# When a group's inputs are split, and which engine makes the low parts, in the second feed-forward of a fused diffusion step

## The chip, the cores and the metric

The kernel runs on one core of a Trainium2 chip. A core has a matrix engine (TensorE, PE in the profile; its weight loads are listed as PEld), VectorE (DVE), ScalarE (ACT), GpSimd (POOL), and SyncE (SP), whose queue issues the DMAs. The metric is the device time of one whole execution in microseconds (us); lower is better.

## The reference

One step of a backbone with a single layer (width 1024, hidden width 2816) for 1024 latent and 128 context tokens. All of it is float32. Of the layer, only the last part matters here:

```
x = x + 0.5 * m[2] * swiglu(modulate(x, norm_g[0], m[0], m[1]), *ffn1)
x = x + m[5] * token_mixer(modulate(x, norm_g[1], m[3], m[4]), ...)
x = x + 0.5 * m[8] * swiglu(modulate(x, norm_g[2], m[6], m[7]), *ffn2)
y = rmsnorm(x, final_g)

modulate(x, g, shift, scale) = rmsnorm(x, g) * (1.0 + scale) + shift
swiglu(h, w1, w3, w2)        = (silu(h @ w1) * (h @ w3)) @ w2
```

## The kernel before, in words

**Layout and precision.** Activations are held transposed: 128 features on the partitions, 1152 tokens along the free axis, so x is eight tiles x0 to x7. The tokens are cut into four quarters of 288 (`QUARTERS`), worked through in the order 3, 0, 1, 2 (`QORDER`), so the last one is tokens 576 to 863. A float32 product is made of three passes: each operand is split into a high part (a rounded copy, on ScalarE) and a low part (value minus high part, one subtraction on VectorE or GpSimd), and TensorE adds high x high, high x low and low x high (`mm3`, lines 518 to 520). So for every operand there is a copy and a subtraction before TensorE can use it.

**Second feed-forward, up.** The third residual's norm is applied quarter by quarter by `norm` (a generator; the one for the last quarter is `self.tail`). For each of eight feature tiles k it multiplies x by the reciprocal root (L476, DVE), applies gain and shift (L480, ACT), writes the vector to DRAM (L483), copies the high part (L487, ACT) and subtracts for the low part (L488, POOL). The result, an entry vector, lands in the tiles B. The scratch tile `xn` comes from a ring of four tiles of 128x288 with the tag "sl"; the SiLU results of the blocks below come from the same ring. A second ring, `half`, holds six tiles of 128x576 with the tag "xp".

Three plain blocks come first (`plain_block`, f = 0, 1, 2; 128 hidden units each). A block is two weight tiles (j = 0 for w1, j = 1 for w3) times four quarters, 24 matmuls each, in one of three PSUM banks with the tag "up". For j = 0 ScalarE takes the SiLU (L1723), for j = 1 DVE multiplies the two (L1734) and the result is written to DRAM. The weights come through `load_w` and `hl`: DMA, copy on ACT (L350), subtraction on POOL (L351, 128x1024). `hl` has another branch, home="low", in which the subtraction is made on DVE in two halves of 128x512. While the plain blocks run, a generator `sums` builds sums and differences of the entry vectors from DRAM, in tiles of the ring `half` (L1678 to L1681, then L1684 and L1688 on ACT and DVE), which the fast blocks (from f = 3) need: these use a scheme with seven products in place of eight (`PRODUCTS` is their order). In the first block the last quarter is taken last, since its norm is ready last.

**Second feed-forward, down.** The hidden vectors from f = 3 on are taken in pairs and in three groups (`GROUPS`: 2, 3 and 3 pairs). For each group `down_fast` makes four sweeps (m = 0 to 3), each of seven products (`down_sweep`; matmuls in L2004). A product takes, for both pairs of quarters, n = 2 or 3 pairs of hidden vectors and three passes, so 12 or 18 matmuls. Its result is emptied from the bank on ACT (L1987, L2007) or DVE (L1989, L1991, L2009); some products start on a bank that an earlier one has filled, after that bank was read. Between products `after()` is called. It brings in, among other work, the splits of the inputs: the generator `down_xs` yields one split at a time (load of 128x576 into a tile of `half`, five ahead; copy on ACT, L1968; subtraction on POOL, L1969, or on DVE for every k = 1). A group with three pairs has 21 splits, three for each product. In the first group's first sweep one split is drawn per product; those of the next group are begun at m = 2 (their first five loads) and all drawn in the last sweep, m = 3:

```
if m == KT // 2 - 1 and not last:
    for _ in range(GROUPS[g + 1][1]):
        next(xg, None)
```

The weights of the sweeps are split by `down_ops` (L1942 on ACT, L1943 on DVE; in the last group also sums on POOL, L1937).

**What sets the order.** The program is written as a sequence of instructions, and a planner at build time puts those of each engine in one queue: among the instructions whose inputs and tiles are free by its own estimate of time, the one written first goes first, unless an instruction is pinned. The queue then runs strictly in that order on the chip. So a place in the program is a priority, not a time.

Of the kernel before, what the change touches and what calls it, by code (L numbers as in the profile page):

```python
# [9 lines left out]
F32 = mybir.dt.float32  # L10
# [9 lines left out]
P = 128  # L20
D = 1024
KT = D // P
# [19 lines left out]
QORDER = [QUARTERS[q] for q in QS]  # L42
# [3 lines left out]
GROUPS = (3, 2), (7, 3), (13, 3)  # L46
# [3 lines left out]
def span(c):  # L50

    return c if isinstance(c, tuple) else (c * CW, (c + 1) * CW)


def segs(c):

    lo, hi = span(c)
    r = []
    if lo < TL:
        r.append((lo, min(hi, TL), 0))  # L60
    if hi > TL:
        r.append((max(lo, TL), hi, 1))
    return r
# [30 lines left out]
class Trunk:  # L94
# [354 lines left out]
    def norm(self, c, i):  # L449

        nc = self.nc
        lo, hi = span(c)
        cs = slice(lo, hi)
        rs = self.rs[:, cs]
        if self.mode != "mix":
            rs = self.bank("ps1", "rsp", hi - lo)
        last = self.mode == "mix"
        if last:
            with self.tc.high_priority(offset=600):
                self.stat_end(c, rs)  # L460
        else:
            self.stat_end(c, rs)
        yield
        for k in range(KT):
            t = self.fp.tile([P, hi - lo], F32, tag=self.nt[0], bufs=self.nt[1], name="xn")
            if last:
                for a, b, s in segs(c):
                    v, th, tl = t[:, a - lo : b - lo], self.xh[k][:, a:b], self.xl[k][:, a:b]
                    g, sh = self.gs[:, i, k, s : s + 1], self.modt[:, 3 * i, k, s : s + 1]
                    rv = rs[:, a - lo : b - lo]  # L470
                    nc.vector.scalar_tensor_tensor(v, self.x[k][:, a:b], g, rv, ALU.mult, ALU.mult)
                    nc.scalar.activation(th, v, AF.Identity, bias=sh)
                    nc.vector.scalar_tensor_tensor(tl, v, sh, th, ALU.add, ALU.subtract)
                yield
                continue
            nc.vector.tensor_mul(t, self.x[k][:, cs], rs)  # L476
            for a, b, s in segs(c):
                v = t[:, a - lo : b - lo]
                g, sh = self.gs[:, i, k, s : s + 1], self.modt[:, 3 * i, k, s : s + 1]
                nc.scalar.activation(v, v, AF.Identity, scale=g, bias=sh)  # L480
            if i == 2:
                q, r, j = self.place(c)
                nc.sync.dma_start(self.hd[r, k % 4][:, 2 * (k // 4) + j], t)  # L483
                th, tl = [v[:, k % 4] for v in self.B[q][k // 4]]
            else:
                th, tl = self.xh[k][:, cs], self.xl[k][:, cs]
            nc.scalar.copy(th, t)  # L487
            nc.gpsimd.tensor_sub(tl, t, th)  # L488
            yield

    def place(self, c):
# [278 lines left out]
    def proj_gate(self, i, p, pair):  # L770
# [16 lines left out]
        def put(cs, s):  # L787
            nc.gpsimd.tensor_mul(s, oT[:, cs], s)
            nc.sync.dma_start(self.orec[p][:, cs], s)

        self.later.append(norm)
        for c in ORDER:
            ps = yield from self.proj_g(w, c)
# [1231 lines left out]
    def down_fast(self, w2, X, xg, ops, made, load_x, load_h, split_h, gm, nxt):  # L2025

        S = [self.tt(F32, "su")[:, :T].rearrange("p (m n) -> p m n", m=4) for _ in range(2)]
        rest = [2, *range(PLAIN[1] + 16, NF)]
        pend, ws = [], []
        self.folds = []  # L2030
        for g, (f, n) in enumerate(GROUPS):
            new = {} if g else X
            last = g == len(GROUPS) - 1
            for m in range(KT // 2):
                if m == 2 and not last:
                    new = {}
                    xg = self.down_xs(g + 1, new)
                    next(xg)
                k, raws, xa = 0, [], []
                if g and m in (1, 2):  # L2040
                    xa += [(i, load_x(i)) for i in range(4 * g + 2 * m - 6, 4 * g + 2 * m - 4)]

                def after():
                    nonlocal k
                    if xa and k in (2, 5):
                        i, t = xa.pop(0)
                        for v in range(2):
                            c = ts(v, 2 * QW)
                            self.nc.vector.tensor_add(self.x[i][:, c], t[:, c], self.x[i][:, c])
                    if m == KT // 2 - 1 and not last:  # L2050
                        for _ in range(GROUPS[g + 1][1]):
                            next(xg, None)
                    elif last:
                        for _ in range((0, 0, 1, 2, 1, 1, 1)[k]):
                            self.folds.pop(0)()
                        if m == KT // 2 - 1:
                            if k in (0, 2):
                                raws.append(load_h(k // 2))
                            if k in (1, 3):
                                pend.append(split_h(*raws.pop(0)))  # L2060
                            if k in (0, 2):
                                ws.append(self.load_w(w2[k // 2], 1, D, home=partial(self.tt, F32R)))
                    elif not g and not m:
                        next(xg, None)
                    k += 1

                self.down_sweep(g, m, X, ops, made, gm, S, after)
            X = new
        assert not made
        for f in rest[:2]:  # L2070
            pend.append(split_h(*load_h(f)))
        fs, hs = zip(*pend[:2])
        assert not self.folds
        self.down_group(w2, fs, hs, gm, ws)
        for f in rest[2:]:
            pend.append(split_h(*load_h(f)))
        fs, hs = zip(*pend[2:])
        self.down_last(w2, fs, hs, gm, nxt)

    def ffn_fast(self, l, gm, nxt):  # L2080

        nc = self.nc
# [7 lines left out]
        sums, ops, made = iter(()), iter(()), []  # L2090
        steps = iter(()) if l else self.whole()
        for f in range(plain):
            ws = self.pre[f] if l == 0 and f < 2 else [self.load_w(self.a["w13"][l, f, j], KT, P) for j in range(2)]
            if f == 2 - l:
                for _ in steps if l == 0 else self.tail:
                    pass
                sums = self.sums()
            if f == plain - 1:
                ops = self.fast_ops(l, range(plain, NF))
            n = 0  # L2100

            def after():
                nonlocal n
                if l and f == 0:
                    next(self.tail, None)
                elif f == 1 - l:
                    if n % 2 == 0:
                        next(steps, None)
                elif f:
                    next(sums, None)  # L2110
                if f == plain - 1 and n > 7 and n % 2:
                    made.append(next(ops))
                n += 1

            self.plain_block(l, f, ws, after)
# [4 lines left out]
        pend, ws, raws = [], [], []  # L2120
# [38 lines left out]
        xg = self.down_xs(0, X) if l else None  # L2159
# [52 lines left out]
        for f in range(2, NF):  # L2212
            pend.append(split_h(*load_h(f)))
            if f % 2 and f < NF - 1:
                fs, hs = zip(*pend[:2])
                self.down_group(w2, fs, hs, gm, ws or [load_w2(v) for v in fs])
                pend, ws = pend[2:], None
# [127 lines left out]
```

## Time and profile before

| | us |
|---|---|
| median of three runs | 2864.26 |
| lowest and highest | 2857.67, 2866.94 |
| the profiled execution | 2864.89 |
| its span in the profile | 2862.8 |
| idle of TensorE in front of the matmuls of the plain blocks (L518, L519) | 5.3 |
| idle of TensorE in front of the matmuls of the sweeps (L2004) | 8.2 |

The profile lists for each engine its instructions with the line of the kernel, the tiles written and read ("out<-in"), and the shape. A row of waits names the instruction that waited, the one that released it, the sum in us, the number of waits and the longest. A row of a window gives for a stretch of time the busy time of each engine and the number of its instructions, then the clock granted to TensorE as a share of full speed, the share of the DMA engines that was busy, and GB/s. Matmuls are pipelined: each is listed with about 0.29 us, but one starts every 0.13 us.

### The profile page before, as it was taken

The numbers are of one execution on the slowest core, as the hardware profiler recorded it, in microseconds if no ns is written. First come the engines' busy times: TensorE is split into PE (matmuls) and PEld (weight loads), VectorE is DVE, ScalarE is ACT, GpSimd is POOL, SyncE is SP. The second block draws the span as 40 slices with busy tenths as digits, with TensorE's granted clock in tenths as the row PEclk, the third lists the DMA queues.
The fourth block names the chain that finished last, engine by engine and source line by source line (L and its number), as shares of the span: only waits on it lengthen the run. The fifth ranks groups of instructions, "written<-read, shape, count | busy, mean of one in ns | idle before, by whom it ended". The sixth has DMA issues, their size and how long they took to land. (4 is left out here: it accounts for less than half of the span.)

```text
span 2862.8 us, 55873 instructions
## 1 busy us (share of the span) xinstructions
PE 2776.7 (97%) x21222; PEld 2644.7 (92%) x21222; DVE 2027.9 (71%) x4439; ACT 1333.4 (47%) x2740; POOL 961.3 (34%) x1003
## 2 busy tenths in 40 slices
PE   8999999999999999999999999989999999999998
PEld 7999999999989999889998777689989999999997
DVE  7867777677678787876356677855765676568885
ACT  6523332321176677666545777721642322235332
POOL 0133322544222222222144444532442443423450
PEclk9999999999999999999999999999999999999999
DMA  6743433743112111112512001263543443446631
GB/s 258 225 129 118 132 122 123 261 165 118 62 65 69 49 57 35 54 46 74 174 45 75 16 16 30 82 215 97 181 153 116 147 152 122 126 146 209 204 100 67
DMA packets 218940, 331.76 MB, mean 116 GB/s; under 512 B 24048, under 2 KB 142768, under 8 KB 218672
## 3 DMA queue, kind: packets, MB, share of 16 engines
q1 hardware_dynamic: 218672, 328.20, 35.3%
q8 instruction: 167, 2.74, 0.4%
q14 instruction: 101, 0.83, 0.1%
HBM read 244.93 MB, written 83.18 MB: 115 GB/s over the span
## 5 line engine op out<-in xcount | busy, mean ns | idle before, releaser
L1804 PE MATMUL b<-xo,wo 128*128 128x288 f32 x3552 | 483.6, 295 | 1.1 <-DVE wo L1779 1.1
L1804 PEld LDWEIGHTS b<-xo,wo 128*128 128x128 f32 x3552 | 475.5, 188 | 1.3 <-DVE wo L1779 1.3
L1804 PE MATMUL b<-bh,wo 128*128 128x288 f32 x1776 | 366.4, 295 | 0.0
L518 PE MATMUL mm<-xh,wh 128*128 128x384 f32 x984 | 345.6, 351 | 14.1 <-DVE sg L795 5.2
L520 PE MATMUL mm<-xh,wl 128*128 128x384 f32 x984 | 335.1, 341 | 0.0
L519 PE MATMUL mm<-xl,wh 128*128 128x384 f32 x984 | 334.5, 340 | 0.0
L1804 PEld LDWEIGHTS b<-bh,wo 128*128 128x128 f32 x1776 | 289.2, 188 | 0.1
L547 DVE SCALAR_TENSOR_TENSOR x<-dn,modt,x 128x256 f32<-128x256 f32 (+4 forms) x472 | 225.5, 498 | 88.3 <-PE dn L520 87.0
L1804 PE MATMUL b<-bl,wo 128*128 128x288 f32 x888 | 262.2, 295 | 0.0
L1778 ACT CAST wo<-raw 128x512 fp32r<-128x512 f32 x185 | 114.8, 621 | 204.7 <-issue 85.6
L518 PEld LDWEIGHTS mm<-xh,wh 128*128 128x128 f32 x984 | 187.1, 190 | 22.9 <-DVE sg L795 6.8
L519 PEld LDWEIGHTS mm<-xl,wh 128*128 128x128 f32 x984 | 187.1, 190 | 1.1 <-issue 0.3
L2004 PE MATMUL d<-xd,wd 128*128 128x288 f32 x1344 | 179.7, 295 | 8.2 <-DVE x L1991 4.0
L520 PEld LDWEIGHTS mm<-xh,wl 128*128 128x128 f32 x984 | 187.3, 190 | 0.0
L2004 PEld LDWEIGHTS d<-xd,wd 128*128 128x128 f32 x1344 | 178.5, 188 | 9.3 <-ACT wd L1942 3.6
L1779 DVE TENSOR_TENSOR wo<-raw,wo 128x512 fp32r<-128x512 f32 x185 | 127.4, 689 | 70.9 <-ACT wo L1778 68.0
L390 DVE SCALAR_TENSOR_TENSOR junk<-wada,cb 128x512 bf16<-128x512 f32 x224 | 163.9, 732 | 8.6 <-DMA wada<-in_w_aT 7.8
L1516 POOL TENSOR_TENSOR ehl<-e,ehl 128x512 fp32r<-128x512 f32 x93 | 122.0, 1317 | 141.4 <-ACT ehl L1514 75.9
L1804 PEld LDWEIGHTS b<-bl,wo 128*128 128x128 f32 x888 | 167.3, 188 | 0.0
L351 POOL TENSOR_TENSOR wl<-raw,wh 128x1024 fp32r<-128x1024 f32 (+2 forms) x48 | 95.3, 1986 | 161.6 <-ACT wh L350 142.7
L518 PE MATMUL ps<-bh,wh 128*128 128x288 f32 (+1 forms) x448 | 137.5, 307 | 8.1 <-DVE sl L1734 3.8
L1779 DVE TENSOR_TENSOR wo<-ws,wo 128x512 fp32r<-128x512 f32 x74 | 71.1, 961 | 101.6 <-ACT wo L1778 100.6
(456 smaller groups left out, 7133.6 us busy)
## 6 DMA issues: line engine op xcount, KB each, us to landing
raw<-in_w SPq DMA_DIRECT2D x148, 256.0 KB, 3.4
wada<-in_w_aT SPq DMA_DIRECT2D x112, 256.0 KB, 3.0
raw<-in_w SPq DMA_DIRECT2D x42, 512.0 KB, 3.8
raw<-in_w_in SPq DMA_DIRECT2D x41, 512.0 KB, 3.4
xr<-xd SPq DMA_DIRECT2D x56, 288.0 KB, 3.9
hr<-hs SPq DMA_DIRECT2D x26, 576.0 KB, 5.9
hb<-hd SPq DMA_DIRECT2D x44, 288.0 KB, 3.8
hs<-et SPq DMA_DIRECT2D x84, 144.0 KB, 2.3
```

The lines of the kernel that those rows point to most:

```text
L351: pin((eng or self.nc.gpsimd).tensor_sub(wl, raw, wh))
L390: nc.vector.scalar_tensor_tensor(junk, ws[n % 2], 1.0, cs[s], ALU.mult, ALU.mult, accum_out=o)
L518: pin(nc.tensor.matmul(ps, wh, xh, start=start and i == 0, stop=False))
L519: pin(nc.tensor.matmul(ps, wh, xl, start=False, stop=False))
L520: pin(nc.tensor.matmul(ps, wl, xh, start=False, stop=stop and i == n - 1))
L547: nc.vector.scalar_tensor_tensor(self.x[m][:, a:b], ps[:, a - lo : b - lo], self.modt[:, gm, m, s : s + 1], self.x[m][:, a:b], ALU.mult, A ...
L1516: eng.tensor_sub(el, e, eh)
L1778: nc.scalar.copy(wh, src[i])
L1779: nc.vector.tensor_sub(wl, src[i], wh)
L1804: nc.tensor.matmul(ps, w[:, k], x[:, k, :QW], start=first, stop=last, skip_group_check=home != i)
L2004: nc.tensor.matmul(ps, w[:, k], xv, start=start, stop=stop, skip_group_check=home != i)
```

## The change

It has three parts, all in the second feed-forward.

```
 norm():
-        last = self.mode == "mix"
+        last, tail = self.mode == "mix", i == 2 and c == QORDER[-1]
...
-            t = self.fp.tile([P, hi - lo], F32, tag=self.nt[0], bufs=self.nt[1], name="xn")
+            if tail:
+                t = self.half("xn")[:, : hi - lo]
+            else:
+                t = self.fp.tile([P, hi - lo], F32, tag=self.nt[0], bufs=self.nt[1], name="xn")
...
-            nc.gpsimd.tensor_sub(tl, t, th)
+            (nc.vector if tail else nc.gpsimd).tensor_sub(tl, t, th)

 down_fast(), after():
+                    if m == KT // 2 - 1 and not last or g and not m:
+                        for _ in range(2):
+                            next(xg, None)
                     if m == KT // 2 - 1 and not last:
-                        for _ in range(GROUPS[g + 1][1]):
-                            next(xg, None)
+                        pass
                     elif last:
                         for _ in range((0, 0, 1, 2, 1, 1, 1)[k]):

 ffn_fast():
-            ws = self.pre[f] if l == 0 and f < 2 else [self.load_w(self.a["w13"][l, f, j], KT, P) for j in range(2)]
+            ws = self.pre[f] if l == 0 and f < 2 else [
+                self.load_w(self.a["w13"][l, f, j], KT, P, home="low" if l and f else None) for j in range(2)
+            ]
```

(a) For the last quarter the eight entry vectors of the second feed-forward take their scratch tile from the ring `half` and no longer from "sl", and their low parts are subtracted on VectorE. (b) The low parts of the weights of its plain blocks 1 and 2 (four tiles) are made on VectorE, in two halves each. (c) The next group's 21 splits are drawn two per product: fourteen in the last sweep of a group, and the other seven after the first four products of the next group's first sweep. The computation stays the same.

## Prediction

> **What bounds the kernel now.** I read the page first, then the waits of TensorE, then windows of the two places that the diff touches, then each engine's timeline around every gap found there.
>
> ```profile
> span 2862.8 us, 55873 instructions
> PE 2776.7 (97%) x21222; PEld 2644.7 (92%) x21222; DVE 2027.9 (71%) x4439; ACT 1333.4 (47%) x2740; POOL 961.3 (34%) x1003
> 2649.77 50.40 PE L2004 MATMUL d<-xd,wd 128*128 128x288 f32 x378
> ```
>
> TensorE is the bound (97%). An unhindered 128x288 matmul costs 50.40/378 = 0.133 us; no matmul is added or removed, so the change can only win back what TensorE loses. That is little, and it lies in two places: the three plain blocks (2070.0 to 2158.8) and the twelve sweeps (2582.8 to 2770.8).
>
> ```profile
> 2070.00:2089.60 19.60, 19.60 (x148) 19.42 (x146) 9.79 (x19) 14.74 (x27) 13.77 (x15) 1.00 0.61 200
> 2089.60:2104.00 14.40, 12.30 (x61) 10.67 (x60) 8.21 (x17) 8.38 (x20) 7.70 (x11) 0.76 0.55 174
> 2104.00:2126.00 22.00, 21.07 (x159) 20.83 (x158) 21.45 (x39) 10.83 (x27) 9.14 (x7) 1.00 0.62 188
> 2126.00:2158.80 32.80, 30.51 (x216) 30.28 (x217) 13.29 (x25) 7.64 (x17) 6.19 (x6) 0.95 0.22 71
> PE d L2004 <- DVE x L1991: 4.0, 3, 2.5
> PE d L2004 <- ACT x L1987: 2.1, 1, 2.1
> PE d L2004 <- DVE su L2009: 2.0, 1, 2.0
> ```
>
> In the four windows the columns are the length, then busy time and count of PE, PEld, DVE, ACT, POOL, then the granted clock. The first passes 148 matmuls in 19.6 us, 0.1324 each. At that rate the other three would need 8.1, 21.1 and 28.6 us; they take 14.4, 22.0 and 32.8. So the plain blocks lose 6.3 + 0.9 + 4.2 = 11.4 us. The sweeps' waits are the last three rows: 8.1 us. All that can come back is 19.5 us, 0.7%.
>
> **Part (a): the entry vectors of the last quarter.** TensorE reaches them at 2089.6 and stumbles from one to the next (in a timeline: start, length, what it did, and in brackets the idle time before it and what ended that):
>
> ```profile
> 2090.36 0.37 PE L518 MATMUL ps<-bh,wh 128*128 128x288 f32 x1 [0.59 <-DVE sl L1734]
> 2081.42 0.82 DVE L476 TENSOR_TENSOR xn<-x,rsp 128x288 f32<-128x288 f32 x2
> 2088.12 0.46 DVE L476 TENSOR_TENSOR xn<-x,rsp 128x288 f32<-128x288 f32 x1 [4.22 <-DMA hs<-sl]
> 2100.00:2101.00 1.00, 1.00 (x6) 1.00 (x5) 0.78 (x2) 0.00 (x0) 0.00 (x0) 0.50 0.15 14
> L476 DVE TENSOR_TENSOR xn<-x,rsp 128x288 f32<-128x288 f32 x12 | 5.2, 451 | 8.7 <-DMA hs<-sl 4.2 <-POOL wq L1867 1.9 <-POOL bl L488 1.5
> L480 ACT ACTIVATE xn<-xn,modt,gs 128x288 f32<-128x288 f32 x13 | 7.8, 622 | 5.8 <-DVE xn L476 5.8
> L487 ACT CAST bh<-xn 128x288 fp32r<-128x288 f32 x14 | 5.5, 423 | 0.0
> L488 POOL TENSOR_TENSOR bl<-xn,bh 128x288 fp32r<-128x288 f32 x15 | 12.8, 876 | 5.5 <-ACT bh L487 4.4 <-DMA wq<-in_w 0.9
> ```
>
> The third entry vector (L476 at 2088.12) waited 4.22 us for the write-out of an SiLU tile: entry vectors and SiLU results share the ring of four "sl" tiles. That ring, not an engine, paces them. In own tiles (the ring of six "xp") the pace is ScalarE's, 0.622 + 0.423 = 1.05 us a vector at most. DVE starts the first at 2081.4 as now and ScalarE follows about 1 us later; eight end by about 2082.4 + 8 x 1.05 = 2090.8, while TensorE needs the eighth at 2089.6 + 7 x 3 x 0.133 = 2092.4. The low part costs DVE 0.45 (as L476, same size, two inputs) in place of POOL's 0.88: 8 x 0.45 = 3.6 us more on an engine that is busy 9.79 of 19.6 us here, so hidden; without that cover it would be late by those 3.6. The write to DRAM (L483) stays with each vector, in the same place of SP's queue. The seventh and eighth vector wait for the first two "xp" tiles; that costs little at this pace. Of the 6.3 us I leave 0.8: **gain 5.5**, bounds 3 and 6.3.
>
> Half of this term is clock: the window row shows 0.50 granted at 2100, with six matmuls in a microsecond, though the longest single gap before it was the 0.59 us of the first row. The Trainium skill ("TensorE: Matmul & The Clock Gate", table "Why this matters for your kernels") asks only for gaps under about 3 us; by that rule the clock would have stayed full, and the term would be about 3 us smaller. The trace here disagrees with it.
>
> **Part (b): low parts of two blocks' weights, and the queue of VectorE.**
>
> ```profile
> PE ps L518 <- DVE sl L1734: 3.8, 3, 2.2
> 2080.92 2.66 POOL L351 TENSOR_TENSOR wl<-raw,wh 128x1024 fp32r<-128x1024 f32 x1 [1.86 <-issue]
> 2103.28 2.41 POOL L351 TENSOR_TENSOR wl<-raw,wh 128x1024 fp32r<-128x1024 f32 x1 [4.38 <-ACT wh L350]
> 2108.20 2.61 POOL L351 TENSOR_TENSOR wl<-raw,wh 128x1024 fp32r<-128x1024 f32 x1
> 2121.52 2.40 POOL L351 TENSOR_TENSOR wl<-raw,wh 128x1024 fp32r<-128x1024 f32 x1 [10.71 <-ACT wh L350]
> 2103.91 4.00 DVE L1688 TENSOR_TENSOR xo<-hd,xo 128x288 fp32r<-128x288 f32 x4
> 2117.80 1.56 DVE L1688 TENSOR_TENSOR xo<-hd,xo 128x288 fp32r<-128x288 f32 x4
> L1779 DVE TENSOR_TENSOR wo<-raw,wo 128x512 fp32r<-128x512 f32 x2 | 1.4, 692 | 10.4 <-ACT wo L1778 10.4
> hb<-hd SPq DMA_DIRECT2D x44, 288.0 KB, 3.8
> ```
>
> TensorE waits 3.8 us in all for L1734, which empties its banks and is queued on DVE behind the sums (L1678 to L1688); 0.6 of it was in the entry stage. Four low parts of sums (L1688) take 4.00 us while POOL works at a weight's low part (L351), 1.56 us otherwise: a POOL pass takes 2.4 us from DVE. Moved, a low part costs DVE 2 x 0.692 = 1.38. Three of the four passes (2103, 2108, 2121) fall into the sums: 3 x 2.4 = 7.2 us of stretch go, 4.1 of work come. The one at 2080.9 has beside it L476, which takes no longer for it (0.82 for two): there only 1.4 are added, in DVE's free time. POOL is relieved; the copy on ScalarE and the weights' load stay. Against it: (a) brings TensorE here 5.5 us sooner, and the sums must start later in their own terms, since their first six tiles of "xp", filled ahead now, go to the entry vectors; a new load takes 3.8 us to land (the last row: the sums' loads, 288 KB each, issue to landing). So DVE ends the sums some 3 to 4 us sooner and TensorE asks 5.5 us sooner. With the order of DVE's queue unchanged, waits would grow by about 2; with L1734 sorted further ahead, as TensorE's earlier arrival suggests, they go. Bounds of the 5.1 us at stake here (0.9 + 4.2): worse by 2, better by 4. I take a **gain of 1.5**, nearer the middle, because both rows that decide (stretch and arrival) move by similar amounts.
>
> **Part (c): the splits over two sweeps.** A sweep has seven products of 18 matmuls: 18 x 0.133 = 2.39 us each (12 and 1.6 in the first group). Today all 21 splits of the next group are written within the last sweep, three per product; then 14, and seven after the first four products of the next sweep.
>
> ```profile
> 2626.72 0.67 ACT L1968 CAST xd<-xr 128x576 fp32r<-128x576 f32 x1 [1.44 <-DMA xr<-xd]
> 2627.30 1.04 ACT L1987 ACTIVATE x<-d,modt 128x160 f32<-128x160 f32 x3
> 2640.07 1.83 DVE L1969 TENSOR_TENSOR xd<-xr,xd 128x576 fp32r<-128x576 f32 x1
> 2642.28 0.93 DVE L1991 SCALAR_TENSOR_TENSOR x<-d,modt,x 128x288 f32<-128x288 f32 x2
> 2705.65 1.91 DVE L1969 TENSOR_TENSOR xd<-xr,xd 128x576 fp32r<-128x576 f32 x1 [0.55 <-ACT xd L1968]
> 2709.18 0.81 DVE L2009 TENSOR_TENSOR su<-d,su 128x288 f32<-128x288 f32 x2
> 2723.86 1.33 PE L2004 MATMUL d<-xd,wd 128*128 128x288 f32 x8 [2.51 <-DVE x L1991]
> 2725.00:2730.00 5.00, 5.00 (x40) 5.00 (x39) 4.76 (x11) 1.03 (x2) 1.45 (x2) 1.00 0.36 116
> L1968 ACT CAST xd<-xr 128x576 fp32r<-128x576 f32 x42 | 28.1, 680 | 21.3 <-DMA xr<-xd 12.4 <-DVE x L2049 5.9 <-PE d L2004 2.2
> L1969 POOL TENSOR_TENSOR xd<-xr,xd 128x576 fp32r<-128x576 f32 x28 | 46.5, 1680 | 77.9 <-ACT xd L1968 49.1 <-PE d L2004 28.3 <-DMA xr<-xd 0.5
> 2582.86 42.34 PE L2004 MATMUL d<-xd,wd 128*128 128x288 f32 x319
> 2639.83 1.45 POOL L1969 TENSOR_TENSOR xd<-xr,xd 128x576 fp32r<-128x576 f32 x1 [0.47 <-ACT xd L1968]
> xr<-xd SPq DMA_DIRECT2D x56, 288.0 KB, 3.9
> ```
>
> The first group is 336 matmuls, so it ends at 2582.9 + 336 x 0.133 + 2.1 = 2629.7; the second, 504, at 2629.7 + 67.0 + 1.2 = 2697.9. The first three pairs of rows are one pattern: a split (L1968, L1969) stands in a queue ahead of the instruction that empties TensorE's bank (L1987, L1991, L2009), and TensorE waits behind both. The 2.1 us wait: the split held ScalarE 1.44 us for its data, ahead of L1987. The 1.2 us wait (L1991's three are 4.0 = 1.2 + 0.3 + 2.51): a split of 1.83 us ahead of L1991. The 2.0 us wait: L2009, whose first product ended about 9 us earlier (2697.9 + 2.4 = 2700.3), had three splits ahead. After the change the last seven are written behind the results of these first products, so these three waits have no split ahead: 5.3 us. Nothing is late next from the seven themselves at POOL's pace: five of them at 1.68 = 8.4 us within the four products' 9.6, the other two on DVE; two of their loads move with them on SP, 3.9 us to landing. But today's last split ends at 2641.3, and the product that needs it comes near 2629.7 + 6 x 2.39 = 2644.0: a margin of 2.7 us, no more. The 2.8 us that are left (2.51 of them at 2723.9) stand in a stretch in which DVE is full (4.76 of 5.0 right after); and of the 2.0 removed before it I return 1.0 there, since DVE has the same work and less pause. **Gain 4.3**, bounds 2 and 7.
>
> **Sum.** 5.5 + 1.5 + 4.3 = 11.3 us against the profiled execution's 2864.9 (span 2862.8 and 2.1 around it): 2853.6. The three runs have a median of 2864.3, 0.6 lower: **2853.0**. A measurement of this kernel can tell about 0.3%, 8.6 us: faster means under 2855.7, slower over 2872.9.
>
> **Rivals.**
> - *VectorE becomes the bound of the plain blocks.* It gets 8 x 0.45 + 8 x 0.69 = 9.1 us of work there, and is at 21.45 of 22.0 in the third window. If L1734 stays behind the sums, (b) loses 2 of waits and 2 of half clock: 5.5 - 4 + 4.3 = 5.8, time 2858.5. For it: 21.45 of 22.0. Against: 7.2 of that is stretch by POOL. Chance 0.15.
> - *The splits don't move.* They run when their tiles and data come, whatever their place in the program; the queue order stays. Gain 5.5 + 1.5 = 7: 2857.3. For it: the wait of 1.44 us for data, not for an engine. Against: the order in the three pairs of rows. Chance 0.15.
> - *All of it comes back*: 6 + 4 + 7 = 17: 2847.3. Chance 0.08.
> - *The half clock does not follow these gaps* (2.51 us of gap left 1.00 after it, in the row at 2725). Then about 3 us stay lost: 2856. Chance 0.05. It is what the clock page's rule above comes to.
> - *Slower: the seven splits come too late.* If they start only with their sweep and go one behind the other: 3.9 + 7 x (0.68 + 1.68) = 20.4 us, while the seventh product asks at 6 x 2.39 = 14.3 and its last part 0.8 later: 5.3 late, at both changes of group 10.6, and two stretches of half clock at 3 us: 16.6, with no gain in (c). Against 7 from (a) and (b): slower by 9.6, 2873.9. It decides from 3.5 us of lateness on. For it: the margin of 2.7 us. Against: loads run five ahead, so the first do not wait for the sweep. Chance 0.07.
>
> **How the numbers follow.** The forecast holds 0.50 (2849 to 2857, by its bounds). Faster: 0.44 of it, all of the full recovery, 0.05 from the edges of the others: 0.57. Slower: 0.07. Same: 0.36. The range 2846.5 to 2861.5 takes in full recovery and the two rivals that halve the gain, and leaves out the slow one and a change of nothing.
>
> **What would show it.** Right: no 4.2 us wait of L476 for a write of hs; clock 1.00 from 2090 to 2104; TensorE past the plain blocks some 7 us sooner; no split ahead of L1987, L1991, L2009 at the two changes of group; no POOL pass of L351 between 2080 and 2125. Wrong: waits for L1734 of more than 3.8 us, waits of L2004 for L1969 or L1968 in the products five to seven, or the three waits of (c) in their old places.

## The result, and the profile after

The changed kernel takes 2856.11 us (median of 13 runs, 2852.00 to 2863.36), the kernel before, beside it on the same chip, 2863.20 (13 runs). The ratio is 0.9979, 95% interval 0.9972 to 0.9987: some 6 us faster (3.7 to 8.0), where 2853.0 and a gain of 11.3 were predicted. The time lies in the predicted range; the gain is under the 0.3% that the prediction set for "faster". The lines that the texts name have moved by 3 (L476 is L479, L488 is L491, L518 is L521, L1678 to L1691 are L1681 to L1694, L1734 is L1737, L1969 is L1972, L2004 is L2007, L2009 is L2012).

Where the time came from is read from the stages' starts in the two traces:

| us | before | after |
|---|---|---|
| start of the plain blocks (code ahead of it untouched) | 2070.0 | 2067.4 |
| three plain blocks | 88.8 | 83.3 |
| fast blocks | 424.1 | 424.1 |
| twelve sweeps | 187.7 | 186.6 |
| rest | 92.2 | 92.3 |
| span | 2862.8 | 2853.6 |

The 9.2 us between the two profiles are 5.5 in the plain blocks, 1.2 in the sweeps, and 2.6 that come from code that is the same in both.

The windows of the plain blocks after (columns as before: length, then PE, PEld, DVE, ACT, POOL, the granted clock, DMA share, GB/s), each from about the same matmul on as its counterpart:

```profile
2087.00:2101.40 14.40, 14.40 (x111) 14.40 (x110) 9.96 (x25) 5.95 (x15) 0.00 (x0) 1.00 0.88 283
2101.40:2123.40 22.00, 21.30 (x161) 21.06 (x159) 18.03 (x43) 9.91 (x24) 9.62 (x8) 1.00 0.63 204
2123.40:2150.70 27.30, 24.01 (x168) 23.78 (x169) 11.05 (x19) 6.38 (x14) 6.01 (x7) 0.94 0.24 84
```

The entry stage is gone as a loss: 111 matmuls in 14.4 us at full clock, where 61 were done before. The last window is still poor. The waits of TensorE after, first in the plain blocks, then in the sweeps:

```profile
PE ps L521 <- DVE sl L1737: 4.0, 2, 2.7
PE d L2007 <- DVE x L1994: 4.6, 5, 2.5
PE d L2007 <- DVE su L2012: 2.0, 1, 2.0
```

L1737 is waited for as much as L1734 was (3.8). In the sweeps, at the first change of group, waits of 2.10 (ScalarE's) and 1.21 us have become 0.94, 0.39 and 0.42; at the second, the 2.0 for L2012 and a longest one of 2.5 stand as before. The timeline at these places:

```profile
2127.57 1.83 POOL L1777 TENSOR_TENSOR raw<-raw 128x256 f32<-128x256 f32 x2
2127.85 0.97 DVE L1684 TENSOR_TENSOR hd<-hb,hd 128x288 f32<-128x288 f32 x1
2128.74 0.97 DVE L1691 TENSOR_TENSOR xo<-hd,xo 128x288 fp32r<-128x288 f32 x1
2130.14 0.61 PE L521 MATMUL ps<-bh,wh 128*128 128x288 f32 x1 [2.72 <-DVE sl L1737]
2694.62 6.74 POOL L1972 TENSOR_TENSOR xd<-xr,xd 128x576 fp32r<-128x576 f32 x4
2696.71 1.67 DVE L1972 TENSOR_TENSOR xd<-xr,xd 128x576 fp32r<-128x576 f32 x1 [0.77 <-ACT xd L1971]
2698.30 1.78 DVE L1946 TENSOR_TENSOR wd<-wr,wd 128x384 fp32r<-128x384 f32 x1
2700.00 0.81 DVE L2012 TENSOR_TENSOR su<-d,su 128x288 f32<-128x288 f32 x2
2700.59 2.63 PE L2007 MATMUL d<-xd,wd 128*128 128x288 f32 x18 [1.96 <-DVE su L2012]
2702.43 0.54 DVE L1946 TENSOR_TENSOR wd<-raw,wd 128x384 fp32r<-128x384 f32 x1
2714.68 1.58 PE L2007 MATMUL d<-xd,wd 128*128 128x288 f32 x10 [2.50 <-DVE x L1994]
```

Two things are to be seen. At the second change of group the order on VectorE has not changed: a split and a weight's low part still stand ahead of L2012 on VectorE, and TensorE waits 1.96 and 2.50 us (2.0 and 2.51 before). And both remaining places have the same look: while POOL works on two inputs, VectorE's instructions with two inputs from the on-chip memory take two to three times as long (L1946 takes 1.78 at 2698 and 0.54 at 2702, L1684 0.97 in place of 0.45), while L2012, one of whose inputs is a bank (two in 0.81 us), is not stretched.

### The profile page after: what moved, and what is told of

It reads as the page before. It is cut to its first block, busy times and chain, and to the rows that moved or that the text cites. A ratio compares the mean times of both kernels' runs of the same rounds, so it can differ in the third digit from the quotient of the medians.

```text
span 2853.6 us, 55855 instructions
## 1 busy us (share of the span) xinstructions
PE 2769.8 (97%) x21222; PEld 2638.7 (92%) x21222; DVE 2026.1 (71%) x4455; ACT 1335.2 (47%) x2740; POOL 953.6 (33%) x991
## 5 line engine op out<-in xcount | busy, mean ns | idle before, releaser
L521 PE MATMUL mm<-xh,wh 128*128 128x384 f32 x984 | 345.8, 352 | 14.6 <-DVE sg L798 6.2
L550 DVE SCALAR_TENSOR_TENSOR x<-dn,modt,x 128x256 f32<-128x256 f32 (+4 forms) x472 | 225.5, 498 | 86.7 <-PE dn L523 85.5
L521 PEld LDWEIGHTS mm<-xh,wh 128*128 128x128 f32 x984 | 186.8, 190 | 23.8 <-DVE sg L798 8.4
L2007 PE MATMUL d<-xd,wd 128*128 128x288 f32 x1344 | 180.2, 295 | 6.6 <-DVE x L1994 4.6
L2007 PEld LDWEIGHTS d<-xd,wd 128*128 128x128 f32 x1344 | 178.6, 188 | 8.1 <-DVE x L1994 3.4
L521 PE MATMUL ps<-bh,wh 128*128 128x288 f32 (+1 forms) x448 | 136.4, 305 | 7.3 <-DVE sl L1737 4.0
L1781 ACT CAST wo<-ws 128x512 fp32r<-128x512 f32 x74 | 45.6, 617 | 202.3 <-POOL ws L1777 196.5
```

What stands on the lines that cost most here:

```text
L521: pin(nc.tensor.matmul(ps, wh, xh, start=start and i == 0, stop=False))
L550: nc.vector.scalar_tensor_tensor(self.x[m][:, a:b], ps[:, a - lo : b - lo], self.modt[:, gm, m, s : s + 1], self.x[m][:, a:b], ALU.mult, A ...
L1781: nc.scalar.copy(wh, src[i])
L2007: nc.tensor.matmul(ps, w[:, k], xv, start=start, stop=stop, skip_group_check=home != i)
```

## Experiments: the parts one by one

All ratios are to the kernel before, timed on the same chip in five rounds. In these kernels the lines are those of before, or of after where the entry vectors' tiles are in.

**Own tiles alone**: of the change only the edit that takes `xn` for the last quarter from `half`.

> The kernel before with one piece of part (a): the last quarter's entry vectors take their scratch tile from the ring "xp"; the low parts stay on POOL. Theory (the ring of four "sl" tiles paced the entry vectors): the plain blocks shrink from 88.8 to about 84 us, the clock stays at 1.00 from 2090 to 2104, the time falls by about 5 us. Rival (the pace was that of POOL's low parts, 0.88 us each, queued behind a 2.66 us pass of L351): the plain blocks stay above 87 us.

Measured: 2862.04 us, ratio 1.0002 (0.9993 to 1.0011); plain blocks 85.3. In its timeline:

```profile
2116.87 2.60 POOL L351 TENSOR_TENSOR wl<-raw,wh 128x1024 fp32r<-128x1024 f32 x1
2117.15 2.64 DVE L1691 TENSOR_TENSOR xo<-hd,xo 128x288 fp32r<-128x288 f32 x1
2121.69 0.40 PE L521 MATMUL ps<-bh,wh 128*128 128x288 f32 x1 [2.62 <-DVE sl L1737]
```

TensorE gets through the entry stage with 1.3 us of waits (2.0 before), and then one single instruction of VectorE, 0.45 us elsewhere, takes 2.64 while a weight's low part runs on POOL; TensorE waits 2.62 behind it. What the tiles win is given back at the passes that part (b) removes. Without (b), (a)'s tiles gain nothing that the times can show (2 us faster to 3 us slower).

**VectorE for the entry vectors alone**: the ring "sl" stays.

```
-            nc.gpsimd.tensor_sub(tl, t, th)
+            (nc.vector if tail else nc.gpsimd).tensor_sub(tl, t, th)
```

> The kernel before with the other piece of part (a): the eight low parts on VectorE, the scratch tiles still from "sl". Theory (ring): the third entry vector still waits about 4 us for a write of hs, the plain blocks stay within 1 us of 88.8. Rival (engine): about 84 us.

Measured: 2860.54 us, ratio 0.9990 (0.9982 to 0.9999); plain blocks 85.5, waits for L1734 4.0. VectorE still waits 3.83 us for a write of the ring, as the theory of the ring had it, and TensorE then waits for a high part, made behind it:

```profile
2090.72 0.53 PE L518 MATMUL ps<-bh,wh 128*128 128x288 f32 x2 [1.35 <-ACT bh L487]
```

But the plain blocks fell by as much as with the tiles, which that theory did not expect. The table further below shows why both lengths say little.

**Low parts of the weights alone** (part (b), `home="low"`).

> The kernel before with part (b) alone: the low parts of the weights of plain blocks 1 and 2 on VectorE. Theory (stretch by POOL goes, work of VectorE comes): the sums end about 3 us sooner, the waits for L1734 fall from 3.8 to under 2, plain blocks 86 to 87 us; the entry stage still loses its 6 us. Rival (VectorE becomes the bound): waits for L1734 of more than 3.8 us, plain blocks over 89 us.

Measured: 2856.63 us, ratio 0.9981 (0.9972 to 0.9989); plain blocks 81.6, less than with the whole change. TensorE's waits there:

```profile
PE ps L519 <- POOL bl L488: 1.9, 1, 1.9
PE ps L518 <- DVE sl L1734: 0.6, 1, 0.6
```

Both theories expected longer plain blocks: 86 to 87, and over 89. With POOL's four passes gone, L1734 is waited for 0.6 us in place of 3.8, and the entry stage, which (b) does not touch, has one wait of 1.9 in place of five of 2.0 in all, so nearly as much. This edit alone is as fast as all three.

**The splits alone** (part (c)).

> The kernel before with part (c) alone. Theory (a place in the program is only a priority: at the second change of group the queues keep their order, at the first they shift by a few places): plain blocks unchanged at 88.8, sweeps 187.7 to about 186.6 us, waits of the sweeps 8.2 to about 6.6, the 2.0 and 2.5 us waits stay. Rival (the prediction): the sweeps fall by 4 us or more.

Measured: 2862.16 us, ratio 0.9996 (0.9988 to 1.0005); plain blocks 88.9, sweeps 186.4. The sum of waits in the sweeps is 6.1 (8.1 before), and the longest, 2.5 for L1991, stays. So (c) is worth 1 to 2 us, as theory had it, by time no more than the measurement can tell.

**The low parts and the splits, without (a)**, and **the changed kernel once more** for the scatter.

> Parts (b) and (c) without (a). Theory: POOL's four passes of 2.4 us are what the plain blocks suffered from, by what they took from VectorE and by standing ahead of the entry vectors' low parts; with them gone, part (a) adds nothing, since the six tiles that it takes were filled with the sums' data ahead of time. Then plain blocks 81 to 82 as with (b) alone, end of the plain blocks within 0.7 us of the changed kernel's, time within 1.5 us of the changed kernel's, so a ratio of 0.9975 to 0.9985. Rival: (a) is worth its predicted 5.5 us by itself and (b) 1.5; then this kernel is 3 to 5 us slower than the changed kernel, ratio 0.999 to 1.000.

> The changed kernel once more, beside the three below, to show what one profiled execution differs from another of the same kernel. The code ahead of the plain blocks is the same in all kernels so far, but they started at 2067.1 to 2070.0; the sweeps of the kernels that leave them alone took 187.7, 188.7, 190.2 and 190.5. If that is scatter, this run's start and sweeps (186.6 in the first profile) differ from the first profile's by 1 to 2 us as well; if it follows from the order of the queues, which is fixed, sweeps come out within 0.5 us of 186.6. Ratio to the kernel before 0.998 either way.

Measured: without (a) 2855.36 us, ratio 0.9971 (0.9960 to 0.9982); the changed kernel 2856.53, ratio 0.9969 (0.9958 to 0.9981). They are equal within the intervals, with plain blocks of 82.2 without (a), so (a) adds nothing that can be told to (b) and (c), and the rival (3 to 5 us slower without (a)) falls. The repetition gave the same kernel a start of the plain blocks at 2069.4 in place of 2067.4 and 84.9 in place of 83.3 for them, but sweeps of 186.2 beside 186.6. So the start scatters by 2 us, as supposed. That the sweeps came out alike hides a difference. The windows of the sweeps (columns as before), for the changed kernel's two profiles, then for the kernel before and for VectorE for the entry vectors alone:

```profile
2574.80:2761.30 186.50, 179.94 (x1345) 178.45 (x1345) 158.37 (x306) 83.75 (x167) 77.15 (x49) 1.00 0.59 185
2578.30:2764.52 186.22, 181.31 (x1346) 179.98 (x1345) 158.21 (x307) 82.91 (x167) 77.58 (x49) 0.99 0.60 185
2582.80:2770.60 187.80, 179.63 (x1347) 178.50 (x1345) 160.13 (x305) 83.44 (x167) 77.04 (x49) 1.00 0.59 183
2576.64:2766.86 190.22, 182.25 (x1347) 181.41 (x1345) 162.33 (x306) 83.24 (x167) 78.05 (x49) 0.98 0.59 181
```

The idle time of TensorE (length less busy time) is 6.6 us in the first profile and 4.9 in the second, which in return ran 3.4 us at half clock. So the idle time of one kernel scatters as well. The last two kernels have the same order of instructions on VectorE, ScalarE and POOL here and nearly the same idle time, 8.2 and 8.0; the second of them ran 6.8 us at half clock, which costs 3.4. So the spread between kernels that leave the sweeps alone (187.7 to 190.5) is half clock for the most part, with some idle time (6.4 to 8.9).

## Experiments: POOL beside VectorE

**The first fast block's weight sums on VectorE**, added to the changed kernel:

```
-                        nc.gpsimd.tensor_tensor(o[:, c], x[:, c], y[:, c], op)
+                        (nc.gpsimd if j or not l else nc.vector).tensor_tensor(o[:, c], x[:, c], y[:, c], op)
```

> The changed kernel with the weight sums of the first fast block (eight instructions of 128x256) on VectorE in place of POOL. Theory: the last two waits for L1737 (1.27 and 2.72 us) and the half clock after them come from these POOL passes at 2123.8 to 2129.4, which stretch VectorE's sums from 0.45 to 0.98 us each. Then L1737 is waited for less than 1.5 us in all, no clock of 0.5 near 2131, and the plain blocks take 79 to 80.5 in place of 83.3; ratio about 0.9968. Rival: VectorE is simply full, and eight more instructions of some 0.4 us, 3.2 us in all, come ahead of L1737 in place of the stretch; then the waits stay at 3 to 5 us and the plain blocks at 83 or more.

Measured: 2852.10 us, ratio 0.9961 (0.9948 to 0.9974); plain blocks 82.1. The wait of 2.72 us is gone, since the same sums now take 0.45 each; six of the moved instructions run at 2130 to 2132, behind L1737, in 0.37 each. But the wait before it grew from 1.27 to 2.17, since there VectorE had waited for loads of its sums. The theory is right on the place, but its plain blocks (79 to 80.5) are some 2 us too short. By the times the step from the changed kernel is not certain, as the intervals overlap (0.9958 to 0.9981 there).

**All low parts of the second and third groups' splits on VectorE**, added to the changed kernel:

```
-            (nc.vector if k == 1 else nc.gpsimd).tensor_sub(lo, raw, hi)
+            (nc.vector if k == 1 or g else nc.gpsimd).tensor_sub(lo, raw, hi)
```

> The changed kernel with all low parts of the splits of the second and third group on VectorE (28 more of them there, none on POOL). Theory: at the second change of group VectorE is late because POOL's six passes of 1.68 us stretch it (0.54 to 1.8 us for a weight's low part), and the planner does not know of the stretch; on VectorE a low part takes about 0.93, so its work stays about the same in sum but nothing is stretched: the two waits at the change (1.96 and 2.50) fall below 2 us together, sweeps 183.5 to 185.5. Rival: what counts is how many instructions stand in VectorE's queue ahead of L2012 and L1994; it gets more of them, and the waits of L2007 on VectorE rise from 6.6 to over 9 us, sweeps 188 or more.

Measured: 2849.14 us, ratio 0.9950 (0.9938 to 0.9963); sweeps 181.3 (186.6), waits 1.2 us in all (6.6). At the second change of group TensorE runs on without a gap. Groups of VectorE in the changed kernel (after the bar: busy us, then mean ns of one):

```profile
L1972 DVE TENSOR_TENSOR xd<-xr,xd 128x576 fp32r<-128x576 f32 x21 | 27.8, 1324 | 7.7 <-ACT xd L1971 7.7
L1946 DVE TENSOR_TENSOR wd<-wq,wd 128x384 fp32r<-128x384 f32 (+1 forms) x27 | 21.0, 780 | 7.4 <-ACT wd L1945 7.3
L1946 DVE TENSOR_TENSOR wd<-wr,wd 128x384 fp32r<-128x384 f32 (+1 forms) x27 | 19.4, 720 | 2.4 <-ACT wd L1945 2.2
L1946 DVE TENSOR_TENSOR wd<-raw,wd 128x384 fp32r<-128x384 f32 (+1 forms) x24 | 16.0, 665 | 0.1
```

and in this one, with its TensorE across the change of group:

```profile
L1972 DVE TENSOR_TENSOR xd<-xr,xd 128x576 fp32r<-128x576 f32 x49 | 40.5, 849 | 10.9 <-ACT xd L1971 10.9
L1946 DVE TENSOR_TENSOR wd<-wr,wd 128x384 fp32r<-128x384 f32 (+1 forms) x27 | 15.8, 585 | 2.1 <-ACT wd L1945 2.0
L1946 DVE TENSOR_TENSOR wd<-wq,wd 128x384 fp32r<-128x384 f32 (+1 forms) x27 | 15.4, 572 | 5.5 <-ACT wd L1945 5.3
L1946 DVE TENSOR_TENSOR wd<-raw,wd 128x384 fp32r<-128x384 f32 (+1 forms) x24 | 13.5, 564 | 0.3
2691.39 1.42 DVE L1972 TENSOR_TENSOR xd<-xr,xd 128x576 fp32r<-128x576 f32 x2
2689.82 30.44 PE L2007 MATMUL d<-xd,wd 128*128 128x288 f32 x224
PE 2770.2 (97%) x21222; PEld 2639.0 (93%) x21222; DVE 2026.2 (71%) x4483; ACT 1333.1 (47%) x2740; POOL 900.5 (32%) x963
```

VectorE makes 28 more low parts for 12.7 us (27.8 to 40.5), and its weights' low parts become cheaper by 11.7 (56.4 to 44.7): its busy time is 2026.2 us in all, and was 2026.1. POOL is relieved of 53 us, and it cost VectorE nothing. The rival, that the number of instructions in VectorE's queue counts, falls.

**The same edit on the kernel before**, without any of the three parts.

> The kernel before with one edit: the low parts of the splits of the second and third group all on VectorE, the splits themselves still drawn three per product in the last sweep. Theory: POOL's passes stretched VectorE and that alone made the sweeps wait; the spreading over two sweeps (c) is worth little beside it. Then the sweeps' waits fall from 8.1 to 3 or less and the sweeps take 182 to 184 (187.7 before), plain blocks as before (88 to 90), ratio 0.9975 to 0.9985. Rival: 21 low parts in one sweep of 17 us are too many for VectorE, and it is the spreading that makes room for them; then the waits stay at 6 or more and the sweeps at 186 or more.

Measured: 2856.96 us, ratio 0.9975 (0.9966 to 0.9985); sweeps 181.7. Their waits:

```profile
PE d L2004 <- ACT x L1987: 1.3, 1, 1.3
PE d L2004 <- DVE su L2009: 1.2, 1, 1.2
PE d L2004 <- DVE x L1991: 0.2, 1, 0.2
```

With all 21 splits still in one sweep the sweeps are nearly as short as with (c) and this edit together (181.3), and the time is that of the whole change. What made TensorE wait at the second change of group was the stretch of VectorE by POOL and not the place of the splits: 4.9 us of waits before, 4.8 in the changed kernel, none here. At the first change it is the other way round: 3.3 us before, 2.5 here with POOL relieved, 1.8 in the changed kernel with the splits spread, 0.8 with both.

**All five edits**; then **without (a)**; then **with (a)'s engine but not its tiles**. Each has (b), (c) and both moves to VectorE.

> The changed kernel with both moves to VectorE (the first fast block's weight sums and the splits of the second and third group). If the two gains add up: 4 us for the first and 7.4 for the second below the changed kernel by the medians (2852.1 and 2849.1 beside 2856.5), 1.2 to 2.8 and 5 by the stages: plain blocks 80 to 82, sweeps 181 to 182, ratio 0.994. If the sums only moved a wait to an earlier place (1.27 to 2.2 us there, by loads of the sums), it is no better than the splits' move alone: 0.995.

> As the kernel with both moves, but without part (a): the entry vectors of the last quarter in the old ring, their low parts on POOL. Theory: (a) takes six tiles from the sums, whose loads then come late (waits of 1.7, 1.2 and 0.3 us for them on VectorE, and L1737 behind); without it the sums are ahead and L1734 is hardly waited for, but one wait of 1.8 us for POOL's low part of an entry vector stays. Plain blocks 81 to 82, ratio 0.994, the same as with (a) to 0.0005. Rival: (a) is worth 3 us once POOL is out of the way, and this one is slower than the kernel with all five by so much (0.995).

> As the last one, but with the entry vectors' low parts on VectorE, in the old ring: the half of (a) that takes no tile from the sums. Theory: the wait of 1.8 us for POOL's low part goes with its half clock, and the sums keep their six tiles filled ahead: plain blocks 79 to 80.5, the least of all, sweeps 181 to 182, ratio 0.9935. Rival: the ring of four tiles paces the entry vectors, as the prediction had it; then TensorE waits at them for about the same 1.8 us and this kernel equals the last one.

Measured: all five 2846.98 us, ratio 0.9938 (0.9924 to 0.9952); without (a) 2849.97, 0.9950 (0.9938 to 0.9963); with VectorE but the old ring 2846.68, 0.9940 (0.9927 to 0.9952). The first and the last are the fastest kernels of this study, some 17 us under before, and by the ratios 8 to 12 under the changed kernel. The one without (a) is 3 us slower by its median, which is its rival's number, though the intervals overlap: with POOL relieved, a half of (a) seems to pay. VectorE's half is enough for it, since the last kernel, which has only that half, has the shortest plain blocks, 78.7, as its theory expected (a little under its 79); the tiles alone beside both moves were not run. There VectorE still waits for a write of the ring, and TensorE hardly feels it:

```profile
2088.32 0.45 DVE L476 TENSOR_TENSOR xn<-x,rsp 128x288 f32<-128x288 f32 x1 [2.58 <-DMA hs<-sl]
2093.24 0.54 PE L518 MATMUL ps<-bh,wh 128*128 128x288 f32 x2 [0.54 <-ACT bh L487]
PE ps L518 <- DVE sl L1734: 0.6, 1, 0.6
PE ps L518 <- ACT bh L487: 0.5, 1, 0.5
```

The tiles have a price: with them VectorE waits 5.2 us for loads of the sums in the changed kernel, and 5.4 with all five edits; without them 0.7 with the low parts alone and 1.3 in the last kernel:

```profile
DVE hd L1682 <- DMA hb<-hd: 3.5, 4, 1.7
DVE hd L1681 <- DMA hb<-hd: 1.7, 1, 1.7
```

(these are the changed kernel's, 2087 to 2131), and of the last one:

```profile
DVE hd L1679 <- DMA hb<-hd: 1.3, 1, 1.3
```

**What one profile of the plain blocks can say.** The idle time of TensorE is the length less its busy time; the time at a clock of 0.50 is summed over windows of 1 us.

| kernel | plain blocks | idle | at half clock | sweeps |
|---|---|---|---|---|
| before | 88.8 | 5.3 | 10.2 | 187.7 |
| splits' low parts on VectorE alone | 85.5 | 5.0 | 3.4 | 181.7 |
| splits alone | 88.9 | 8.2 | 3.4 | 186.4 |
| own tiles alone | 85.3 | 5.5 | 3.4 | 188.7 |
| VectorE for the entry vectors alone | 85.5 | 5.4 | 3.4 | 190.2 |
| low parts of the weights alone | 81.6 | 2.6 | 3.4 | 190.5 |
| low parts and splits | 82.2 | 3.0 | 3.4 | 186.9 |
| after, first and second profile | 83.3, 84.9 | 4.3, 4.5 | 3.4, 6.8 | 186.6, 186.2 |
| after, and first weight sums moved | 82.1 | 3.0 | 3.4 | 187.9 |
| after, and splits' low parts moved | 81.5 | 2.5 | 3.4 | 181.3 |
| all five | 79.4 | 1.9 | 0 | 181.0 |
| without (a) | 81.7 | 2.5 | 3.4 | 180.4 |
| VectorE, old ring | 78.7 | 1.1 | 0 | 182.7 |

The first three rows of the table are kernels with the same plain blocks: none of their edits is there, and VectorE, ScalarE and POOL run the same instructions in the same order. Their windows, in the order of the table, show what one profile differs from another:

```profile
2070.01:2158.80 88.79, 83.46 (x580) 81.19 (x579) 52.73 (x97) 41.58 (x89) 36.78 (x38) 0.94 0.46 145
2069.25:2154.79 85.54, 80.59 (x580) 78.32 (x579) 52.72 (x97) 41.59 (x89) 36.84 (x38) 0.98 0.47 151
2068.32:2157.24 88.92, 80.71 (x580) 78.55 (x579) 52.80 (x97) 41.67 (x89) 36.96 (x38) 0.98 0.45 145
```

Idle time scatters from 5.0 to 8.2 us, and half clock from 3.4 to 10.2. Each half of (a) alone has an idle time (5.5, 5.4) within that, and so shows no gain there: the 3.3 to 3.5 us by which they undercut the kernel before are its two further pieces of half clock, (10.2 - 3.4) / 2 = 3.4. What (b) gives is more than the scatter: 2.5 to 3.0 us of idle time in three profiles without (a), against 5.0 to 8.2 in the three without any edit there.

## Why the prediction was right, and where it was wrong

The place and the direction were right, and the size to some 5 us; the shares of the parts were not.

- **Reading of the bound: right.** No kernel here did more than win back waits of the plain blocks and the sweeps and the half clock behind them. The best won 17 us by the medians, and the prediction's total that can come back was 19.5.
- **(a), 5.5 us: wrong step, "That ring, not an engine, paces them", and a gain that did not stay.** In the changed kernel the entry stage runs as predicted, without a gap and at full clock. But the ring was only one of two causes. TensorE's waits in that stage were 2.0 us before, 1.3 with own tiles alone, 1.9 with VectorE alone (1.35 of it for a high part behind the ring), 1.9 with (b) alone (POOL's low part), 0.5 with VectorE, the old ring and both moves, and none with both halves. So POOL held the entry vectors up as well, and either half alone left most of the waits. What was won there was lost again: TensorE waits 4.0 us for L1737 later, and own tiles alone gave a ratio of 1.0002, the whole change no more than (b) and (c) alone. The cost named for the tiles, sums that start later, is real (5.2 us of waits for their loads), and that is where the gain went.
- **(b), 1.5 us: mis-sized, the largest error to the other side.** Alone it is worth 5.4 us by the medians' ratio (0.0019 of 2863; interval 3.1 to 8.0), 2.8 by TensorE's idle time, the rest clock and scatter. The stretch that the step worked out (7.2 us go) was sound: VectorE's work in the plain blocks fell from 52.7 to 50.9 us although 5.5 us of low parts came to it, so 7.3 went. The step that failed set it against TensorE's arrival 5.5 us sooner, which is (a)'s gain and did not stay. What (b) is worth on top of (a) no run shows.
- **(b)'s queue: the 4.0 us of waits that remained.** "With L1734 sorted further ahead ... they go" was not so. It stood behind sums that were late for two reasons: their loads, and POOL's weight sums of the first fast block (L1777), a stretch that the prediction had not priced. Their move to VectorE took the wait of 2.72 away.
- **(c), 4.3 us: wrong step, "so these three waits have no split ahead".** At the first change of group the waits fell from 3.3 us to 1.8 (2.1 to 4.2 in the four profiles without (c) in which POOL makes low parts in all groups, 1.2 to 1.9 in the five with it); at the second, the 2.0 stayed with the same split ahead of L2012. That is the rival "the splits don't move", given 0.15, and it held for one change of two. The profiles give 2.5 us: sweeps of 187.7, 188.7, 190.2 and 190.5 without (c), mean 189.3, and 186.6, 186.2, 186.4, 186.9 and 187.9 with it, mean 186.8. Of these, 1.7 are idle time (means of 7.8 and 6.2); the rest is about half clock, five pieces of 3.4 us in the four profiles without (c) and two in the five with it, which no run ties to (c). Alone (c) gave a ratio of 0.9996.
- **(c)'s cause: wrong at the second change.** The pairs of rows were read as order of the queue. The splits of 1.83 and 1.91 us on VectorE in the quoted rows were themselves stretched: 0.71 is what one takes undisturbed (two in 1.42). The prediction had used this very effect in (b), with the number, and did not look for it in the sweeps. Moving the rest to VectorE took the second change's waits away without (c).
- **The last condition, slower by seven late splits: did not come.** No wait of L2007 for a split's low part is in the changed kernel's list.
- **The sum.** That it stayed within some 5 us is in part luck: (a) came to nothing that can be told, and (b) alone to about what (a) was to bring. 7.0 us were forecast in the plain blocks and 4.3 in the sweeps; 5.5 and 1.2 by the two profiles, where 3.4 of the 5.5 are half clock (10.2 less 3.4, halved). The profiled pair differs by 2.6 us more from code that is the same in both.

What stays open: why the planner leaves the splits in place at one change and not at the other was not tried, nor what decides how many pieces of half clock a profile has. The 2.6 us ahead of the plain blocks are open as well.

## What to carry to other kernels

Before you reorder a queue, compare the same instruction's duration at that place and elsewhere: where an instruction takes twice its usual time while POOL runs, its place need not be what makes it late, and moving POOL's two-input work to VectorE can cost VectorE nothing. Where two edits work on one wait, run each alone and both, since the gain of one can be the other's, and a ring of tiles taken for one use is missed by another. And split a stage's time into idle time and half clock before you compare two single profiles: one piece of half clock is 1.7 us here, as large as most edits, and the idle time of the same plain blocks lay between 5.0 and 8.2 us in three profiles.

## What the runs showed of the hardware that was not expected

**VectorE against POOL.** One instruction of VectorE took 2.64 us in place of 0.45 beside a POOL pass of 2.60, and ended 0.3 us after that pass: it did not share, it stood still. The Trainium skill ("SBUF — State Buffer", section "Who interferes with whom") says that an instruction of VectorE with two inputs in the on-chip memory contends with a GpSimd instruction that reads it, that one with at most one such input does not, and that the ports that the two engines share are an exclusive lock. The trace agrees (2.64 and 2.60), and also for one input: L2012, whose other input is in a bank, took 0.81 us for two with POOL at work.

**The clock.** Half clock came in pieces. In the plain blocks it was 3.4 us in ten of the fourteen profiles, 6.8 in one, 10.2 in the kernel before, none in two. The mean clock of the whole plain blocks shows it, for the changed kernel's second profile and for all five edits:

```profile
2069.37:2154.24 84.87, 80.39 (x581) 79.58 (x579) 51.54 (x114) 41.61 (x89) 23.27 (x26) 0.96 0.51 166
```

```profile
2068.45:2147.85 79.40, 77.47 (x580) 76.86 (x579) 50.42 (x120) 41.45 (x89) 18.02 (x20) 1.00 0.56 177
```

0.04 of 84.87 us is 3.4 lost, two pieces of 3.4 at half clock; the second row has none. The Trainium skill ("TensorE: Matmul & The Clock Gate", section "What's actually happening") tells of a free-running activity window of 4096 cycles, about 3.4 us, and the pieces are whole multiples of that. Which gap sets it off is not a matter of its length alone: after a gap of 2.15 us (splits' low parts on VectorE alone, at 2132) the clock stayed full, after gaps of at most 0.49 us and 1.5 in sum at 2089 to 2093 in the same kernel it fell:

```profile
2089.00:2093.00 4.00, 2.77 (x14) 1.88 (x13) 1.89 (x5) 3.18 (x8) 2.03 (x3) 1.00 0.54 174
2093.00:2097.00 4.00, 3.51 (x13) 3.06 (x13) 2.65 (x4) 3.35 (x9) 3.92 (x7) 0.57 0.78 267
2132.00:2136.00 4.00, 3.55 (x26) 3.55 (x27) 2.06 (x5) 2.03 (x5) 0.00 (x0) 1.00 0.25 89
2132.45 0.40 PE L518 MATMUL ps<-bh,wh 128*128 128x288 f32 x1 [2.15 <-DVE sl L1734]
```

In the first row TensorE started 14 matmuls in 4 us, where 30 fit. So a row of short gaps can cost more than one long one.
